# Low parts of the first MLP weights on another engine, modulation dots at other steps, and another form of the last squares and the final norm

## The chip, the cores and the metric

The kernel runs on one core of a Trainium2 chip. The metric is the device time of one execution in microseconds (us). The kernel before the change was timed three times: 2294.85, 2296.27 and 2297.2 us, median **2296.27 us**.

A core has engines that work beside one another, each through its own queue of instructions in order: TensorE (PE: matmuls; PEld: its weight loads), VectorE (DVE: elementwise work), ScalarE (ACT: activations, copies, scalings), GpSimd (POOL: elementwise work) and SyncE (SP), from whose queue the DMA transfers here are issued.

## The reference

A trunk of two layers over one sequence of 1024 tokens with 1024 channels, all in float32. The first layer mixes tokens by latent attention, the second by an mLSTM; each is followed by a gated MLP. Cut to what the change touches:

```python
D_MODEL, SEQ, DEPTH, D_FF, CONV_W = 1024, 1024, 2, 2816, 3
c_act = jax.nn.silu(c)
for i in range(DEPTH):
    mod = c_act @ mod_w[i] + mod_b[i]              # 6 x 1024 numbers
    sh_a, sc_a, g_a, sh_f, sc_f, g_f = split(mod, 6)
    h = rms_norm(x) * (1 + sc_a) + sh_a
    y = mla_mixer(h, ...) if i % 2 == 0 else mlstm_mixer(h, ...)
    x = x + g_a * y
    h = rms_norm(x) * (1 + sc_f) + sh_f
    x = x + g_f * conv_ffn(h, ffn_w_up[i], ffn_conv_w[i], ffn_conv_b[i], ffn_w_down[i])
return rms_norm(x, final_norm)                      # gain of 1024 numbers

def conv_ffn(h, w_up, conv_w, conv_b, w_down):
    a, g = split(h @ w_up, 2)                       # 2 x 2816 channels
    a = causal depthwise convolution of width 3 over tokens (a) + conv_b
    return (gelu(a) * g) @ w_down
```

## The kernel before

**Layout.** Activations lie transposed: 128 channels on the partitions, 8 tiles (KT) for the 1024 channels, and the tokens in two halves of 512 (HS). `x` is the residual stream, `h` the normed and modulated input of an MLP.

**Products.** Every float32 product is made of three matmuls (`mm3`, L174, with its matmuls on L178, L179 and L180): high part of the weight by high part of the operand, high by low, low by high. A weight is split by `wop` (L943): ACT copies it into `whi` (L948), and then DVE or POOL subtracts this from the weight into `wlo` (L949); the caller names the engine.

**The MLP's up projection** (`mlp`, L925). The 22 tiles of channels are 22 groups `g`. Each group computes its two halves (a, before the convolution, and g, the gate) for both halves of tokens in seven products instead of eight, in the manner of Strassen. A product is a step `k` of 12 matmuls, with the function that makes its weight and the function that runs it in the table `steps`. Its operands are B11 and B21 (parts of `h` itself), B22, and T1 to T4 (sums and differences of parts of `h`, made by `operands_second`, whose DVE rows are on L886, in two steps of 128x1024). The steps:

- 1: weight straight from the loaded tile `ra`, into the bank `pa`, copied into `a1` by ACT;
- 2: weight `ra` (second half), added into `a1` by DVE;
- 5: weight the sum `s` (L962), into the bank `pd`, copied by ACT into `g2` (L1017);
- 3: weight a difference `t` (L966 and L967), into `pd`, copied into `a2`;
- 6: weight `s` itself, onto `pa`, added by DVE into `a2` (L1029); the convolution `conv` (ACT L988, DVE L989 and L990, ACT L991) follows;
- 7: weight another difference `t` (L971), onto `pa`, added by DVE into `g2` (L1036);
- 4: weight from the loaded tile `rg`, onto `pa`, out.

The first four groups (`g["again"]`, AHEAD = 4) are run apart: first steps 1 and 2 of all four, for which `h` of the first half of tokens is enough, then, by pairs of groups, steps 5, 3, 6, 7 and 4, which need the T operands. The other 18 groups follow one another in the order 5, 1, 7 of the group before, 2, 4 of the group before, 3, 6. This is the loop; a list `seq` holds all steps of an MLP (28 for the first four groups, 126 for the rest), and the weight of a step is made some steps ahead of its product. Before the change the low parts of steps 1, 2, 4, 6 and 7 are made on POOL, those of 3 and 5 on DVE, in all groups. The loaded weight tiles `raw` have 4 buffers, the tiles `wraw` with `s` and `t` have 2. Rows called `wsum` are parts of the latter.

**The modulation's dots.** Both layers' modulation is a product of a vector with a matrix. Row tiles of `mod_w` of 512 KB are loaded on SP's queue (L214, two buffers `mraw`), and DVE multiplies each by `crow` with an accumulated sum (`mod_dot`, L202), one column of the result each. Some of these dots are fed into the first MLP by its hook `extra`, called with the number `i` of the step: one dot at every third step, from step 0 to step 144.

**The down projection** (`d_run`, L1146) runs seven products per group in the same manner into the banks `da` and `db`; `gate_x` (L287, row L291) adds each result with its gate into `x` on DVE. In the last group the squares of the finished tiles are summed (`Squares`, L222: ACT squares, DVE adds, L240). The last product of the last group is done in one piece of 512 columns in the first MLP, and in two pieces of 256 columns in the second one.

**The norms.** `rstd_later` (L262) counts matmul triples (`mm3` counts down a list): after a first number of triples, `rstd_cols` (L242) sums the squares over the channels by small matmuls with ones (`st`, one per 128 tokens, L247), DVE scales them (`var`, L251), and POOL takes them to the power -1/2 (L252); after a second number, `to_rows` (L255) spreads the result over the partitions by four transposes (`rb`, L259). Then a function of the caller uses `rb`: `norm_mod` makes `h` of the second layer (a DVE row `nt`, an ACT row, a DVE row per tile), `final` makes the output: one DVE instruction per tile of 128 channels (L1600, x times `fn`, the final norm's gain, times `rb`), and one store on SP's queue for each two tiles. For the final norm the two pairs of numbers are WF = (6, 22) and WF_RSTD = (5, 8), each for the first and the second half of tokens.

**What sets the order.** The functions issue instructions in program order, and a scheduler with priorities places them on the engines; those in `tc.high_priority()` go ahead of what else is ready.

## Time and profile before

| | before |
|---|---|
| median of three timed runs | 2296.27 us |
| the profiled execution's own time | 2297.02 us |
| its span on the core | 2295.3 us |
| its mean granted TensorE clock | 0.979 of full speed |
| HBM read, written | 220.49 MB, 44.47 MB |
| ACT `whi` L948 of `raw` tiles and others, x252 | 146.4 us |
| POOL `wlo` L949 of `raw` tiles, x228 | 341.6 us, 1507 ns each |
| DVE `wlo` L949, x136 | 104.5 us, 773 ns each |

How to read it: busy times are the sums of an engine's instructions in the profiled execution, and the engines overlap. A row with "[7 <-POOL wlo]" says that the engine stood for 7 us ahead of that instruction, until POOL had made `wlo`. In rows, out<-in names the tile that is written and those that are read, then the shape on 128 partitions, and xN counts instructions. Windows are counted in us from the start of the span. The rows on which the prediction rests stand in it.

### The profile page before, as it was taken

The numbers are of one execution on the slowest core, as the hardware profiler recorded it, in microseconds if no ns is written. First come the engines' busy times: TensorE is split into PE (matmuls) and PEld (weight loads), VectorE is DVE, ScalarE is ACT, GpSimd is POOL, SyncE is SP. The second block draws the span as 40 slices with busy tenths as digits, with TensorE's granted clock in tenths as the row PEclk, the third lists the DMA queues.
The fourth block names the chain that finished last, engine by engine and source line by source line (L and its number), as shares of the span: only waits on it lengthen the run. The fifth ranks groups of instructions, "written<-read, shape, count | busy, mean of one in ns | idle before, by whom it ended". The sixth has DMA issues, their size and how long they took to land. (4 is left out here: it accounts for less than half of the span.)

```text
span 2295.3 us, 28811 instructions
## 1 busy us (share of the span) xinstructions
PE 2198.5 (96%) x10489; PEld 1824.8 (80%) x10489; DVE 1698.2 (74%) x2457; ACT 1023.6 (45%) x1784; POOL 756.3 (33%) x550
## 2 busy tenths in 40 slices
PE   8989999998999999999999999999899999999997
PEld 6778888886788888777878878978678888877786
DVE  7876777679988888899972634365776666679987
ACT  5355555445444444443443423344544444453332
POOL 3221111243443343432233222234543333342222
PEclk9999999999999999999999999999999999999998
DMA  7411334762554444642122111135242222245122
GB/s 290 146 47 61 105 98 134 264 204 79 183 161 151 147 147 147 202 147 85 59 97 79 56 46 56 33 125 174 62 128 91 88 83 83 83 151 210 48 74 74
DMA packets 104830, 269.46 MB, mean 117 GB/s; under 512 B 12208, under 2 KB 15984, under 8 KB 104688
## 3 DMA queue, kind: packets, MB, share of 16 engines
q1 hardware_dynamic: 104688, 267.62, 35.8%
q8 instruction: 83, 1.36, 0.3%
q14 instruction: 59, 0.48, 0.1%
HBM read 220.49 MB, written 44.47 MB: 115 GB/s over the span
## 5 line engine op out<-in xcount | busy, mean ns | idle before, releaser
L949 POOL TENSOR_TENSOR wlo<-raw,whi 128x512 fp32r<-128x512 f32 (+1 forms) x228 | 341.6, 1507 | 563.8 <-ACT whi L948 556.6
L171 POOL TENSOR_TENSOR wlo<-wraw,whi 128x1024 fp32r<-128x1024 f32 x64 | 156.4, 2448 | 303.5 <-ACT whi L170 253.2
L948 ACT ACTIVATE whi<-raw 128x512 fp32r<-128x512 f32 (+1 forms) x252 | 146.4, 604 | 220.5 <-PE pb L179 54.5
L949 POOL TENSOR_TENSOR wlo<-wsum,whi 128x512 fp32r<-128x512 f32 x88 | 153.6, 1748 | 245.9 <-ACT whi L948 245.9
L180 PE MATMUL pa<-T,wlo 128*128 128x512 f32 x528 | 207.5, 394 | 14.5 <-POOL wlo L949 14.5
L178 PE MATMUL pa<-T,whi 128*128 128x512 f32 x528 | 208.2, 395 | 9.1 <-DVE a L1029 5.3
L179 PE MATMUL pa<-T,whi 128*128 128x512 f32 x528 | 207.6, 394 | 0.7 <-DVE T L886 0.7
L948 ACT ACTIVATE whi<-wsum 128x512 fp32r<-128x512 f32 (+1 forms) x224 | 134.7, 617 | 163.4 <-PE pa L179 50.3
L178 PE MATMUL da<-U,whi 128*128 128x512 f32 (+1 forms) x364 | 140.7, 386 | 3.2 <-DVE x L291 3.2
L179 PE MATMUL da<-U,whi 128*128 128x512 f32 (+1 forms) x364 | 139.9, 384 | 0.0
L180 PE MATMUL da<-U,wlo 128*128 128x512 f32 (+1 forms) x364 | 139.3, 384 | 0.0
L180 PEld LDWEIGHTS pa<-T,wlo 128*128 128x128 f32 x528 | 99.7, 189 | 37.7 <-POOL wlo L949 15.3
L178 PEld LDWEIGHTS pa<-T,whi 128*128 128x128 f32 x528 | 99.6, 189 | 35.6 <-DVE g L1036 4.6
L170 ACT ACTIVATE whi<-wraw 128x1024 fp32r<-128x1024 f32 x67 | 70.7, 1059 | 126.3 <-PE op L179 53.1
L988 ACT ACTIVATE ct<-a,cols 128x512 f32<-128x512 f32 x88 | 70.9, 811 | 124.6 <-DVE a L1010 70.9
L949 DVE TENSOR_TENSOR wlo<-wsum,whi 128x512 fp32r<-128x512 f32 (+1 forms) x136 | 104.5, 773 | 19.6 <-ACT whi L948 18.6
L179 PEld LDWEIGHTS pa<-T,whi 128*128 128x128 f32 x528 | 99.3, 188 | 23.1 <-DVE T L886 1.6
L991 ACT ACTIVATE ct<-ct 128x512 f32<-128x512 f32 x88 | 55.5, 631 | 127.3 <-DVE ct L990 127.2
L1098 DVE TENSOR_TENSOR U<-q,U 128x1024 fp32r<-128x1024 f32 x84 | 104.1, 1258 | 6.4 <-ACT U L1097 5.7
L180 PE MATMUL db<-U,wlo 128*128 128x512 f32 x264 | 103.1, 392 | 1.7 <-DVE wlo L949 1.7
L178 PE MATMUL db<-U,whi 128*128 128x512 f32 x264 | 103.8, 393 | 0.0
L179 PE MATMUL db<-U,whi 128*128 128x512 f32 x264 | 103.1, 391 | 0.0
(361 smaller groups left out, 6380.6 us busy)
## 6 DMA issues: line engine op xcount, KB each, us to landing
raw<-in_wf SPq DMA_DIRECT2D x96, 512.0 KB, 4.0
wraw<-in_w SPq DMA_DIRECT2D x67, 512.0 KB, 3.6
mraw<-in_mod_w SPq DMA_DIRECT2D x56, 512.0 KB, 4.3
ud<-ct SPq DMA_DIRECT2D x88, 256.0 KB, 2.6
q<-ud SPq DMA_DIRECT2D x88, 256.0 KB, 4.4
raw<-in_wd SPq DMA_DIRECT2D x32, 512.0 KB, 6.2
pa<-in_mod_w SPq DMA_DIRECT2D x24, 512.0 KB, 3.8
xd<-x SPq DMA_DIRECT2D x48, 256.0 KB, 2.7
```

The source lines that it names most:

```text
L170: act.activation(hi, raw, AF.Copy)
L171: (lo_eng or pool).tensor_tensor(lo, raw, hi.bitcast(F32), ALU.subtract)
L178: pe.matmul(ps, lh, rh, start=first, stop=False, skip_group_check=more)
L179: pe.matmul(ps[:, 0:rl.shape[-1]], lh, rl, start=False, stop=False, skip_group_check=more)
L180: pe.matmul(ps, ll, rh, start=False, stop=last, skip_group_check=more)
L948: act.activation(hi, src, AF.Copy)
L949: eng.tensor_tensor(lo, src, hi.bitcast(F32), ALU.subtract)
L988: act.activation(t, a[:, 2:], AF.Identity, bias=col(f"cb{l}", m), scale=cw(m, 2))
L991: act.activation(t, t, AF.Gelu)
L1098: dve.tensor_tensor(lo, w, hi.bitcast(F32), ALU.subtract)
```

## The change

It has four parts.

1. In the four first groups of each MLP, the subtractions for the low parts of steps 4, 6 and 7 are given to DVE instead of POOL: three per group, 12 per MLP, 24 in all. Those of steps 1 and 2, and all of the loop's, stay where they were.
2. In the first MLP the dots are fed in at every second step from step 41 on, instead of at every third from step 0 on. 49 dots take the steps 41 to 137.
3. The last square of the last group (tile 7 of each half of tokens, in both MLPs) is no longer added to the sum by DVE; `Squares.keep` lets it stand, and `rstd_cols` sums it by a second set of small matmuls that accumulates onto the first. All squares of that group are issued with high priority.
4. The final norm's gain `fn` is multiplied into each tile of `x` by ACT (`gain`) right behind its square. `final` then has one DVE instruction for two tiles, x times `rb` broadcast, and a store behind it. The counts WF and WF_RSTD become (4, 8) and (4, 8), and OUTS goes.

```diff
-W0, W0_RSTD, WF, WF_RSTD = (6, 10), (4, 3), (6, 22), (5, 8)
+W0, W0_RSTD, WF, WF_RSTD = (6, 10), (4, 3), (4, 8), (4, 8)
-OUTS = 2
...
+            self.more = []
+
+        def keep(self, x):
+
+            sq = self.sq()
+            act.activation(sq, x, AF.Square)
+            self.more.append(sq)
...
         for t in range(nt):
-            pe.matmul(st[:, t:t + 1], ssq.t[:, t * P:(t + 1) * P], ones, start=True, stop=True)
+            terms = [ssq.t, *ssq.more]
+            for i, v in enumerate(terms):
+                pe.matmul(st[:, t:t + 1], v[:, t * P:(t + 1) * P], ones, start=i == 0, stop=i == len(terms) - 1)
...
         def w_s3(g):
             dve.tensor_tensor(g["t"], g["ra"][:, 0:HS], g["rg"][:, 0:HS], ALU.subtract)
-            return wop(g["t"], pool)
+            return wop(g["t"], dve if g["again"] else pool)
...
+        def eng(g):
+
+            return dve if g["again"] else pool
+
         steps = {1: (w_a, p1), 2: (lambda g: wop(g["ra"][:, HS:], pool), p2), 3: (w_s4, p3),
-                 4: (lambda g: wop(g["rg"][:, HS:], pool), p4), 5: (w_s1, p5), 6: (lambda g: wop(g["s"], pool), p6),
-                 7: (w_s3, p7)}
+                 4: (lambda g: wop(g["rg"][:, HS:], eng(g)), p4), 5: (w_s1, p5),
+                 6: (lambda g: wop(g["s"], eng(g)), p6), 7: (w_s3, p7)}
...
-                        stats[hf, c0].add(xs[hf][:, m, c0:c0 + cw_])
+                        with tc.high_priority():
+                            if p == 3 and op in ("T3", "T4"):
+                                stats[hf, c0].keep(xs[hf][:, m, c0:c0 + cw_])
+                            else:
+                                stats[hf, c0].add(xs[hf][:, m, c0:c0 + cw_])
+                        if scaled is not None:
+                            scaled(xs[hf][:, m, c0:c0 + cw_], m)
...
-    mlp(px, psC, T, 0, u_d[0], pD, done, ((0, HS),), lambda i: piece(mods, i % 3 == 0))
+    mlp(px, psC, T, 0, u_d[0], pD, done, ((0, HS),), lambda i: piece(mods, i >= 40 and i % 2))
...
+    def gain(x, m):
+        act.activation(x, x, AF.Copy, scale=col("fn", m))
+
     def final(x, hf, t0, w, rb):
+
         x = x[:, :, t0:t0 + w]
-        for k in range(KT):
-            dve.scalar_tensor_tensor(x[:, k, :], x[:, k, :], col("fn", k), rb[:, 0:w], ALU.mult, ALU.mult)
-            if k % OUTS == OUTS - 1:
-                k0 = k - OUTS + 1
-                o0 = hf * HS + t0
-                nc.sync.dma_start(out[k0:k + 1, :, o0:o0 + w].rearrange("k p t -> p k t"), x[:, k0:k + 1, :])
+        for k in range(0, KT, 2):
+            v = x[:, k:k + 2, :]
+            dve.tensor_tensor(v, v, rb[:, 0:w].unsqueeze(1).to_broadcast([P, 2, w]), ALU.mult)
+            o0 = hf * HS + t0
+            nc.sync.dma_start(out[k:k + 2, :, o0:o0 + w].rearrange("k p t -> p k t"), v)
...
-    mlp(px, psC, T, 1, u_d[1], pD, done, ((0, 256), (256, 256)))
+    mlp(px, psC, T, 1, u_d[1], pD, done, ((0, 256), (256, 256)), None, gain)
```

The first place is at the T operands of the first MLP, where the first pair of groups goes from step 5 to the steps 3 and 6. DVE's instructions before the change (`T_935` and `T_964` are operands of later steps, `mraw` the dots, `wsum_5119` and `wsum_5192` the sums and differences of the first two groups, `wlo_5215` the low part for step 3):

```order
L886 TENSOR_TENSOR T_935_5020<-x_4670,T_935_5020 128x1024
L202 SCALAR_TENSOR_TENSOR mraw_5066,modc_80<-mraw_5066,crow 128x1024
L949 TENSOR_TENSOR wlo_5215<-wsum_5119,whi_5214 128x512
L886 TENSOR_TENSOR T_964_5168<-x_4106,T_964_5168 128x1024 x2
L967 TENSOR_TENSOR wsum_5192<-raw_5188,wsum_5192 128x512
L971 TENSOR_TENSOR wsum_5119<-raw_5115,raw_5117 128x512
L202 SCALAR_TENSOR_TENSOR mraw_5253,modc_80<-mraw_5253,crow 128x1024
L949 TENSOR_TENSOR wlo_5215<-wsum_5192,whi_5214 128x512
```

And DVE's instructions there in the changed kernel (line numbers are shifted: L886 is L894 now, L949 is L957, L967 is L975, L971 is L979; `wlo_5210` is the low part for step 3, `wlo_5248` that for step 6):

```order
L894 TENSOR_TENSOR T_935_5020<-x_4670,T_935_5020 128x1024
L957 TENSOR_TENSOR wlo_5210<-wsum_5117,whi_5209 128x512
L975 TENSOR_TENSOR wsum_5187<-raw_5183,wsum_5187 128x512
L894 TENSOR_TENSOR T_963_5166<-x_4106,T_963_5166 128x1024 x2
L957 TENSOR_TENSOR wlo_5210<-wsum_5187,whi_5209 128x512
L957 TENSOR_TENSOR wlo_5248<-wsum_5117,whi_5247 128x512
L957 TENSOR_TENSOR wlo_5248<-wsum_5187,whi_5247 128x512
L979 TENSOR_TENSOR wsum_5117<-raw_5113,raw_5115 128x512
```

The dots are gone from here, and two more subtractions stand ahead of L979 (L971 before), the difference for step 7: those of step 6, which POOL made. On PE, at the same place, the products of steps 3 and 6 stood so (`pd` with `B_933`, the operand B22, is step 3; `pa` with `T_934`, the operand T2, is step 6, whose low part `wlo_5256` POOL makes):

```order
L178 MATMUL pa_5050<-T_934_5019,whi_5255 128x512
L178 MATMUL pa_5090<-T_934_5019,whi_5255 128x512
L179 MATMUL pa_5050<-T_934_5019,whi_5255 128x512
L179 MATMUL pa_5090<-T_934_5019,whi_5255 128x512
L180 MATMUL pa_5050<-T_934_5019,wlo_5256 128x512
L180 MATMUL pd_5275<-B_933_5018,wlo_5215 128x512
```

In the changed kernel:

```order
L177 MATMUL pa_5050<-T_934_5019,whi_5247 128x512
L177 MATMUL pa_5088<-T_934_5019,whi_5247 128x512
L178 MATMUL pa_5050<-T_934_5019,whi_5247 128x512
L178 MATMUL pa_5088<-T_934_5019,whi_5247 128x512
L179 MATMUL pd_5267<-B_933_5018,wlo_5210 128x512
L177 MATMUL pd_5267<-B_933_5018,whi_5209 128x512
```

The first matmul there that needs a low part was one of step 6, with `wlo` of POOL; now it is one of step 3, with `wlo` of DVE.

The second place is the loop of the first MLP on DVE, between the add into `a` (L1029, now L1037) and the add into `g` (L1036, now L1044). Before:

```order
L1029 TENSOR_TENSOR a_6386<-a_6386,pa_6293 128x512
L989 SCALAR_TENSOR_TENSOR ct_6409<-a_6386,cols_4405,ct_6409 128x512
L990 SCALAR_TENSOR_TENSOR ct_6409<-a_6386,cols_4405,ct_6409 128x512
L202 SCALAR_TENSOR_TENSOR mraw_6351,modc_80<-mraw_6351,crow 128x1024
L949 TENSOR_TENSOR wlo_6461<-wsum_6458,whi_6460 128x512
L966 TENSOR_TENSOR wsum_6458<-wsum_6458,raw_6482 128x512
L967 TENSOR_TENSOR wsum_6458<-raw_6482,wsum_6458 128x512
L1036 TENSOR_TENSOR g_1115_6284<-g_1115_6284,pa_6293 128x512
```

In the changed kernel, in a later group:

```order
L1037 TENSOR_TENSOR a_6811<-a_6811,pa_6715 128x512
L957 TENSOR_TENSOR wlo_6864<-wsum_6888,whi_6863 128x512
L201 SCALAR_TENSOR_TENSOR mraw_6842,modc_80<-mraw_6842,crow 128x1024
L997 SCALAR_TENSOR_TENSOR ct_6836<-a_6811,cols_4405,ct_6836 128x512
L974 TENSOR_TENSOR wsum_6888<-wsum_6888,raw_6907 128x512
L998 SCALAR_TENSOR_TENSOR ct_6836<-a_6811,cols_4405,ct_6836 128x512
L201 SCALAR_TENSOR_TENSOR mraw_6795,modc_80<-mraw_6795,crow 128x1024
L975 TENSOR_TENSOR wsum_6888<-raw_6907,wsum_6888 128x512
L970 TENSOR_TENSOR wsum_7039<-raw_7037 128x512
L1044 TENSOR_TENSOR g_1169_6708<-g_1169_6708,pa_6715 128x512
```

There are two dots (L202, now L201) between the two adds in place of one, and the sum of the next group (L970, formerly L962) stands there too.

The third place is DVE at the end of the program, behind the last gated adds. Before:

```order
L291 SCALAR_TENSOR_TENSOR x_17066<-da_18273,modc_80,x_17066 128x256
L251 TENSOR_SCALAR var_18757<-st_18754 128x2
L1600 SCALAR_TENSOR_TENSOR x_17097<-x_17097,cols,rb_18623 128x512 x6
L240 TENSOR_TENSOR ssq_18565<-ssq_18565,sq_18725 128x256
L240 TENSOR_TENSOR ssq_18565<-ssq_18565,sq_18738 128x256
L240 TENSOR_TENSOR ssq_18565<-ssq_18565,sq_18751 128x256
L251 TENSOR_SCALAR var_18764<-st_18761 128x2
L1600 SCALAR_TENSOR_TENSOR x_17066<-x_17066,cols,rb_18768 128x256 x8
L1600 SCALAR_TENSOR_TENSOR x_17066<-x_17066,cols,rb_18783 128x256 x8
```

In the changed kernel:

```order
L1623 TENSOR_TENSOR x_17103<-x_17103,rb_18627 128x1024
L259 TENSOR_SCALAR var_18765<-st_18760 128x2
L299 SCALAR_TENSOR_TENSOR x_17072<-da_18261,modc_80,x_17072 128x256
L246 TENSOR_TENSOR ssq_18579<-ssq_18579,sq_18750 128x256
L299 SCALAR_TENSOR_TENSOR x_17072<-da_18279,modc_80,x_17072 128x256
L246 TENSOR_TENSOR ssq_18579<-ssq_18579,sq_18773 128x256
L1623 TENSOR_TENSOR x_17103<-x_17103,rb_18627 128x1024 x2
L1623 TENSOR_TENSOR x_17072<-x_17072,rb_18790 128x2x256 x4
```

`x_17097` (now `x_17103`) is the first half of tokens, `x_17066` (now `x_17072`) the second. Six output rows stood ahead of the last added squares; now the adds come first, and the rows of two tiles follow.

More of the change, by code (lines that the diff above doesn't have):

```diff
@@ L923, in operands_second, with mlp @@
             split_two(T["T4"], k, two(x1, k))
-    def mlp(px, psC, T, l, u_d, pd, done, cols, extra=None):
+    def mlp(px, psC, T, l, u_d, pd, done, cols, extra=None, scaled=None):
         cw = lambda m, j: col(f"cw{l}", m * 3 + j)
```

## Prediction

> **What bounds the kernel now.** First the page's first part, then the waits of TensorE (PE) in total: in us, times, longest.
>
> ```profile
> PE 2198.5 (96%) x10489; PEld 1824.8 (80%) x10489; DVE 1698.2 (74%) x2457; ACT 1023.6 (45%) x1784; POOL 756.3 (33%) x550
> PE pa L180 <- POOL wlo L949: 14.5, 2, 7.3
> PE pd L178 <- ACT g L1017: 1.9, 1, 1.9
> ```
>
> PE sets the time; only its gaps can be won. The largest wait comes twice, once in each MLP, for a low part that POOL computes. Windows tell how much is lost in all around the two places (PE busy with its matmuls in brackets, PEld, DVE, ACT, POOL, granted clock, DMA share, GB/s); the last two rows are the loops of the first and the second MLP.
>
> ```profile
> 540.00:610.00 70.00, 56.15 (x221) 43.63 (x222) 66.85 (x86) 30.89 (x48) 31.42 (x17) 0.90 0.47 154
> 1650.00:1720.00 70.00, 61.40 (x249) 49.37 (x250) 54.83 (x71) 32.75 (x52) 34.33 (x21) 0.90 0.36 113
> 610.00:900.00 290.00, 289.48 (x1264) 236.35 (x1263) 239.41 (x314) 123.80 (x212) 114.29 (x91) 1.00 0.49 154
> 1720.00:2010.00 290.00, 290.00 (x1267) 237.38 (x1266) 196.85 (x243) 124.74 (x212) 108.27 (x90) 1.00 0.27 85
> ```
>
> In a loop a matmul takes 290/1267 = 0.229 us, so 70 us would hold 306. The first window lacks 85 of them (19.5 us), the second 57 (13.0 us). That is all there is to win there. The loops lose nothing, but DVE is busy for 83% of the first one and 68% of the second: the difference is the modulation's dots.
>
> **Why PE waits there.** POOL's, DVE's and PE's rows of the timeline around both waits:
>
> ```profile
> 533.72 14.69 POOL L949 TENSOR_TENSOR wlo<-wsum,whi 128x512 fp32r<-128x512 f32 x2 [15.29 <-ACT whi L948]
> 1643.23 15.30 POOL L949 TENSOR_TENSOR wlo<-wsum,whi 128x512 fp32r<-128x512 f32 x2 [15.28 <-ACT whi L948]
> 543.24 1.22 DVE L886 TENSOR_TENSOR T<-x,T 128x1024 fp32r<-128x1024 f32 x1
> 544.37 1.22 DVE L202 SCALAR_TENSOR_TENSOR mraw<-mraw,crow 128x1024 f32<-128x1024 f32 x1
> 545.52 1.75 DVE L949 TENSOR_TENSOR wlo<-wsum,whi 128x512 fp32r<-128x512 f32 x1
> 1653.89 0.69 DVE L949 TENSOR_TENSOR wlo<-wsum,whi 128x512 fp32r<-128x512 f32 x1
> 546.77 0.79 PE L180 MATMUL pa<-T,wlo 128*128 128x512 f32 x1 [7.21 <-POOL wlo L949]
> 1656.36 0.80 PE L180 MATMUL pa<-T,wlo 128*128 128x512 f32 x1 [7.27 <-POOL wlo L949]
> L949 POOL TENSOR_TENSOR wlo<-wsum,whi 128x512 fp32r<-128x512 f32 x88 | 153.6, 1748 | 245.9 <-ACT whi L948 245.9
> ```
>
> POOL needs 14.7 and 15.3 us for two subtractions that take 1.75 us each on average, while DVE works through its operands (T, B) without a gap. [...]
>
> **The first weights, first MLP.** In the order PE now asks first for the low part of pd, which DVE computes right behind its operands: at 544.37, where the dot stood, plus 0.69 is 545.05, and PE goes on 1.7 us earlier than 546.77. So most of the wait stays: it was POOL's by name, but DVE's queue lies just below it. What remains of the lost 19.5 us is 545.05 - 540 = 5.05 and the slow restart:
>
> ```profile
> 548.00:552.00 4.00, 3.86 (x11) 0.56 0.16 61
> 1692.00:1696.00 4.00, 4.00 (x12) 0.63 0.82 260
> ```
>
> At a clock of 0.56 the four us hold 11 matmuls in place of 17.5, 1.5 us lost; with the stretch before, 2.0. So at most 19.5 - 5.05 - 2.0 = 12.4 us can be won. Behind the wait DVE gets 12 subtractions (three kinds in four groups) at 0.61 us from start to start, 7.3 us, and loses the nine dots up to 610, 13.9 us:
>
> ```profile
> L202 DVE SCALAR_TENSOR_TENSOR mraw<-mraw,crow 128x1024 f32<-128x1024 f32 x9 | 13.9, 1549 | 0.0
> 594.95 0.47 PE L178 MATMUL pa<-T,whi 128*128 128x512 f32 x1 [3.56 <-DVE a L1029]
> ```
>
> Following DVE's rows one by one from 545.05, its add into a is done about 4 us before PE's third product needs it in the second pair of groups: the wait of 3.56 goes, and with it its slow restart. I take **11 us**; lower bound 1.7, the first step alone.
>
> **The first weights, second MLP.** Here DVE's part is done at 1653.89 + 0.69 = 1654.58, again 1.8 us before 1656.36. Of 13.0 us there remain 1654.58 - 1650 = 4.6 and 2.0 of slow restart, so at most 6.4. No dot leaves here and DVE gets 7.3 us more; but its rows beside POOL's (1.7 to 1.8 us for 0.7) shorten, and the wait for g of 1.9 us, whose ACT copy stands behind such a row, should go with its restart at 0.63. Against this, DVE must wait for one weight tile whose buffer its own later subtraction frees (about 0.5 us on PE). I take **5.5 us**; lower bound 1.5.
>
> [...]
>
> **The dots in the first loop.** They now come at every second step from the 41st, not every third from the first. So 49 of them lie in 97 steps of 2.74 us (12 matmuls):
>
> ```profile
> L202 DVE SCALAR_TENSOR_TENSOR mraw<-mraw,crow 128x1024 f32<-128x1024 f32 x36 | 47.7, 1326 | 0.0
> L990 DVE SCALAR_TENSOR_TENSOR ct<-a,cols,ct 128x512 f32<-128x512 f32 x30 | 27.9, 930 | 0.6
> L989 DVE SCALAR_TENSOR_TENSOR ct<-a,cols,ct 128x512 f32<-128x512 f32 x30 | 26.6, 885 | 8.4 <-ACT ct L988 8.4
> L949 DVE TENSOR_TENSOR wlo<-wsum,whi 128x512 fp32r<-128x512 f32 x30 | 24.1, 803 | 5.8 <-ACT whi L948 5.7
> L967 DVE TENSOR_TENSOR wsum<-raw,wsum 128x512 f32<-128x512 f32 x16 | 18.7, 1170 | 0.3
> L962 DVE TENSOR_TENSOR wsum<-raw 128x512 f32<-128x512 f32 x15 | 15.8, 1052 | 23.4 <-POOL wlo L949 23.4
> L966 DVE TENSOR_TENSOR wsum<-wsum,raw 128x512 f32<-128x512 f32 x15 | 12.5, 832 | 0.8 <-DMA raw<-in_wf 0.3
> L1029 DVE TENSOR_TENSOR a<-a,pa 128x512 f32<-128x512 f32 x15 | 10.2, 680 | 3.4 <-PE pa L180 3.4
> L1036 DVE TENSOR_TENSOR g<-g,pa 128x512 f32<-128x512 f32 x14 | 9.6, 683 | 3.6 <-PE pa L180 3.6
> ```
>
> In 290 us that is 53 in place of 36, 17 x 1.33 = 23 us more, so DVE goes from 239 to 262 us, 90%. What hides them is DVE's idle time, 51 us, most of it before wsum. The close place is between the adds into a (L1029) and g (L1036): PE spends four steps, 11.0 us, from the end of the product before the one to the start of the product behind the other. In every second group two dots now lie there; at the means above (L1029, L949, dot, L989, L966, L990, dot, L967, L962, L1036, as the order has them) DVE needs 9.7 us. It fits by 1.3 us, less what DVE waits within. I take **1 us lost**, bounds 0 and 7 (seven such groups, 1 us each). SP gets each dot's load of 512 KB closer; DMA share 0.49 would be some 0.55.
>
> **The last squares.** Where PE sums kept squares there are eight small matmuls in place of four:
>
> ```profile
> 1158.87 1.05 PE L247 MATMUL st<-ones,ssq 128*128 128x1 f32 x8 [0.23 <-DVE ssq L240]
> 1159.79 0.48 PE L178 MATMUL db<-U,whi 128*128 128x512 f32 x1
> ```
>
> Four cost 1159.79 - 1158.87 = 0.92 us, so each norm at the end of the first MLP costs PE 0.9 more, against the 0.23 won. The adds now stand ahead of half of the first half's rows (nt, h), which delays h by up to 3 us with 2.4 in hand. Together **1.5 us lost** (0 to 3).
>
> **The tail.**
>
> ```profile
> 2274.27 0.65 PE L259 MATMUL rb<-ident,rstd 128*128 128x128 f32 x4 [0.76 <-POOL rstd L252]
> 2277.36 0.41 PE L180 MATMUL da<-U,wlo 128*128 128x256 f32 x1
> 2278.53 4.03 DVE L1600 SCALAR_TENSOR_TENSOR x<-x,cols,rb 128x512 f32<-128x512 f32 x6
> 2284.01 1.01 PE L247 MATMUL st<-ones,ssq 128*128 128x1 f32 x4 [5.59 <-DVE ssq L240]
> 2285.58 6.36 DVE L1600 SCALAR_TENSOR_TENSOR x<-x,cols,rb 128x256 f32<-128x256 f32 x16 [0.30 <-PE rb L259]
> 519.89 2.35 DVE L879 TENSOR_TENSOR x<-x,rb 128x1024 f32<-128x1024 f32 x2
> 2280.00:2284.00 4.00, 0.00 (x0) 0.00 (x0) 3.74 (x7) 0.42 (x1) 0.00 (x0) 0.50 0.78 296
> 2288.00:2292.00 4.00, 0.00 (x0) 0.00 (x0) 3.94 (x11) 0.00 (x0) 0.00 (x0) 0.50 1.02 332
> ```
>
> Six output rows stand ahead of the last squares on DVE, hence the 5.59; this order goes. DVE's rows: 8 x 0.67 + 16 x 0.40 = 11.7 us become 4 x 1.14 (by L879, two tiles against PSUM) + 8 x 0.67 = 9.9. But PE gets 0.9 for the first st, and a doubled st (1.7 to 2.0 at half clock, by the row of 1.01) between the last products, so these end at 2280.3, not 2277.6. Then the gate (0.5), the add and one double row (1.5) pass beside the last square and its doubled st, which end at 2283.5; two double rows (2.3) and eight (5.4) end at 2291.2, and the store behind takes as before 2295.3 - 2291.94 = 3.4: 2294.6. The stores alone end little earlier: with the second pair of tiles out at 2282.9, 1.5 MB at 296 / 0.78 = 380 GB/s and 2 MB at 332 need 10.4 us, to 2293.3. **0.7 us won** (3 won to 1.5 lost). The gains are put on by ACT, which works 0.4 of 4 us here.
>
> **Sum**, against the profiled execution's 2297.02: -11 - 5.5 + 1 + 1.5 - 0.7 = -14.7, 2282.3. It stands 0.75 over the median of 2296.27, so the forecast is 2281.6.
>
> **The rivals.** A: *DVE takes the place of POOL.* The waits move to DVE's queue, and only the first steps (1.7 + 1.8) and a bit of the rest are won: -6 + 2, about 2292. For it: DVE is busy for 66.85 of the 70 us of the first window. Against it: 13.9 us of dots leave there. B: *the dots make DVE the bound of the first loop.* Beside POOL a row of DVE can take twice its time (1.75 above for 0.69). If each of the 53 dots takes twice its undisturbed 1.22, DVE needs 239 - 48 + 129 = 320 us in 290; it decides from dots of 1.86 on. PE then loses 30 us, and 2281.6 + 29 = 2311, slower. For it: more DVE rows beside POOL's. Against it: the mean dot stays at 1.33 with POOL busy for 39% of this loop. C: *nothing arrives*, as the weights' DMAs behind the freed buffers come late and give back both places: about 2295. Against it: DMA share 0.47 and 0.36 there, and the dots' loads no longer stand ahead of the weights' in SP's queue, where they hold it for 34 us:
>
> ```profile
> 511.90 34.06 SPq L214 DMA_DIRECT2D mraw<-in_mod_w  x3
> ```
>
> **Chances.** Forecast 0.68, A 0.16, C 0.07, B 0.09. The range takes A in and the larger bounds of the forecast (12.4 + 6.4 + 3 won, nothing lost): 2274.5 to 2292. A change of less than 0.2% (4.6 us) can hardly be told from none. Faster by more than that, under 2291.7: the forecast and near three quarters of A, 0.80; same: the rest of A, C and a mild B, 0.13; slower 0.07.
>
> **What would show it.** In the new profile PE waits for DVE's wlo, not POOL's, 5 to 6 us at 545 and at 1640; no wait for a of 3.6 us; POOL without a row of 14 us; the dots between 620 and 905 with no PE wait over 1 us; the tail's last DVE row some 11 us behind the last product, and stores back to back. A PE wait in each second group of the first loop means B; waits for wlo or raw between 550 and 590 mean A or C.

## The result and the profile after

The changed kernel takes **2314.74 us**, median of seven runs (2305.38 to 2319.17), against 2296.27 us before (seven runs, 2291.38 to 2300.8): ratio 1.0074, 95% interval 1.0052 to 1.0097. It is 0.7% slower, which lies outside the range of 2274.5 to 2292 us and goes against the forecast of 2281.6 us.

The profiled execution has a span of 2314.4 us, 19.1 more than before. The page's first part and PE's largest waits (us in total, times, longest) of the changed kernel:

```profile
PE 2210.5 (96%) x10521; PEld 1836.4 (79%) x10521; DVE 1686.2 (73%) x2464; ACT 1036.7 (45%) x1808; POOL 692.1 (30%) x526
PE pa L177 <- DVE g L1044: 24.8, 8, 3.9
PE pd L179 <- DVE wlo L957: 11.1, 2, 5.5
```

The wait for POOL's low part (14.5 us before) has become one for DVE's, 11.1. A new one stands above it: PE waits for the add into g. The windows of the changed kernel (PE with matmuls, PEld, DVE, ACT, POOL, clock, DMA share, GB/s) show where: the first weights of both MLPs, counted from the same place as before, then the loops.

```profile
542.00:612.00 70.00, 64.56 (x274) 52.44 (x275) 59.03 (x90) 35.85 (x57) 11.05 (x10) 0.95 0.37 122
1677.00:1747.00 70.00, 65.32 (x273) 52.94 (x274) 58.10 (x89) 35.85 (x57) 10.72 (x10) 0.95 0.35 121
620.00:910.00 290.00, 268.36 (x1121) 217.02 (x1121) 226.21 (x309) 109.39 (x186) 104.70 (x82) 0.96 0.49 155
1749.00:2039.00 290.00, 290.00 (x1268) 237.43 (x1267) 197.98 (x244) 124.49 (x212) 108.42 (x90) 1.00 0.27 86
```

In 70 us the first weights now hold 274 and 273 matmuls in place of 221 and 249. But the first loop lost 143 of its 1264, and DVE is busy there for 226 of 290 us, less than the 239 before: it is not full, it waits.

The whole by stages, from DVE's rows in the timeline: from the first low part of B22 to the fifth add into g ("first weights"), from there to the last add into g ("loop"), then to the first ACT row of `C` in the mLSTM, and the second MLP in the same way. In us:

| kernel | first weights 1 | loop 1 | to C | first weights 2 | loop 2 | to the end | median |
|---|---|---|---|---|---|---|---|
| before | 98.5 | 326.7 | 309.8 | 92.5 | 325.7 | 236.3 | 2296.27 |
| changed | 85.9 | **359.2** | 313.3 | 87.0 | 325.7 | 233.9 | 2314.74 |
| e1 dots as before | 91.8 | 326.7 | 313.3 | 87.0 | 325.7 | 234.3 | 2287.7 |
| e2 loads one dot ahead | 86.2 | 356.2 | 313.3 | 87.0 | 325.7 | 233.9 | one run |
| e3 sum on POOL | 86.3 | 339.1 | 313.3 | 88.0 | 325.7 | 233.9 | one run |
| e4 dots spread | 86.4 | 328.2 | 316.7 | 86.8 | 325.7 | 233.9 | 2284.92 |
| e5 sums' tiles taken once | 86.0 | 332.5 | 309.6 | 86.9 | 325.7 | 233.9 | one run |
| e6 half dots | 85.9 | 333.4 | 314.8 | 86.9 | 325.7 | 233.9 | one run |
| e7 dots in order | 87.6 | 332.8 | 312.8 | 86.9 | 325.7 | 233.9 | one run |
| e8 no loads | 86.4 | 332.7 | 311.3 | 87.3 | 325.7 | 233.8 | one run |
| e9 = e4, squares as before | 86.4 | 328.2 | 313.4 | 87.2 | 325.7 | 233.9 | 2281.0 |
| e10 = e9 with e5's tiles | 86.2 | 327.0 | 313.1 | 86.0 | 325.7 | 237.1 | 2279.4 |
| e11 before, dots moved | 90.3 | 349.4 | 309.6 | 92.5 | 325.7 | 236.2 | one run |

The differences of the changed kernel to before, taken before rounding: -12.6, **+32.6**, +3.5, -5.5, 0 and -2.5. With +2.3 up to the first weights and +1.2 between C and the second MLP this makes the 19.1. One stage turned a gain of some 14 us into a loss of 19.

Each row of stages comes from one execution, and executions of the changed kernel differ by up to 14 us. The second loop repeats to 0.1 us in all thirteen kernels, and the first weights of the first MLP to 1.7 us in the ten that have the whole change there. But the part ahead of them took 527.6 to 533.8 us in eight kernels whose differences all lie behind it. So a few us outside the loops and the first weights say little by themselves.

**The place.** It lies between DVE's add into a and its add into g. It comes once in two groups, six times in the loop: 43.5 to 44.7 us for two groups instead of 38.4. DVE's rows of the timeline of the changed kernel at the first of them (start, us, then in brackets the idle time ahead and its releaser; the rows that close the accumulation of a dot are left out):

```profile
667.73 1.21 DVE L201 SCALAR_TENSOR_TENSOR mraw<-mraw,crow 128x1024 f32<-128x1024 f32 x1
...
670.19 0.68 DVE L1037 TENSOR_TENSOR a<-a,pa 128x512 f32<-128x512 f32 x1
670.79 1.19 DVE L957 TENSOR_TENSOR wlo<-wsum,whi 128x512 fp32r<-128x512 f32 x1
674.01 1.23 DVE L201 SCALAR_TENSOR_TENSOR mraw<-mraw,crow 128x1024 f32<-128x1024 f32 x1 [2.04 <-DMA mraw<-in_mod_w]
675.16 0.75 DVE L997 SCALAR_TENSOR_TENSOR ct<-a,cols,ct 128x512 f32<-128x512 f32 x1
675.83 0.68 DVE L974 TENSOR_TENSOR wsum<-wsum,raw 128x512 f32<-128x512 f32 x1
676.43 0.74 DVE L998 SCALAR_TENSOR_TENSOR ct<-a,cols,ct 128x512 f32<-128x512 f32 x1
677.09 1.22 DVE L201 SCALAR_TENSOR_TENSOR mraw<-mraw,crow 128x1024 f32<-128x1024 f32 x1
678.23 0.69 DVE L975 TENSOR_TENSOR wsum<-raw,wsum 128x512 f32<-128x512 f32 x1
681.33 1.74 DVE L970 TENSOR_TENSOR wsum<-raw 128x512 f32<-128x512 f32 x1 [2.41 <-POOL wlo L957]
682.99 0.67 DVE L1044 TENSOR_TENSOR g<-g,pa 128x512 f32<-128x512 f32 x1
```

PE's row behind it, which waits for that add:

```profile
683.81 0.77 PE L177 MATMUL pa<-T,whi 128*128 128x512 f32 x1 [3.84 <-DVE g L1044]
```

Read it from the add into a (670.19) to the end of the add into g (683.66): 13.5 us, of which DVE works 9.0 (forecast: 9.7) and waits 2.04 + 2.41 = 4.45. PE gives 11.0 us between the products, and DVE begins on the add into a about 1.2 us after PE has finished, since a dot, a low part and a difference stand ahead of it. So 11.0 - 9.0 - 1.2 - 4.45 = -3.7, and PE's waits at the six places are 3.25 to 3.85 us. Before the change, the stretch with one dot had the wait for POOL too, and still fitted: from 640.84 to 650.93 it took 10.1 us, of which 2.95 were waits, and PE did not wait. Its last two rows:

```profile
649.64 0.69 DVE L962 TENSOR_TENSOR wsum<-raw 128x512 f32<-128x512 f32 x1 [2.69 <-POOL wlo L949]
650.25 0.68 DVE L1036 TENSOR_TENSOR g<-g,pa 128x512 f32<-128x512 f32 x1
```

The first wait is a matter of order. The rows of the change that were shown ahead of the prediction have it in the numbers of the tiles: `mraw_6842` stands ahead of `mraw_6795`. Of the two dots, the one whose load was issued later runs first, and waits for that load, while the other's has landed. The second wait hangs on it: behind the late dot comes the convolution (L998), ACT's gelu waits for that at the head of ACT's queue, and ACT's copies of the weights and POOL's low part behind it. ACT's and POOL's rows there:

```profile
677.21 0.63 ACT L999 ACTIVATE ct<-ct 128x512 f32<-128x512 f32 x1 [4.86 <-DVE ct L998]
678.74 0.62 ACT L956 ACTIVATE whi<-wsum 128x512 fp32r<-128x512 f32 x1
680.04 1.25 POOL L957 TENSOR_TENSOR wlo<-wsum,whi 128x512 fp32r<-128x512 f32 x1
```

POOL is done at 681.29, and L970, which overwrites what POOL reads, starts at 681.33. Behind each of PE's six waits the clock falls as well. Windows of the changed kernel around the wait of 3.40 us that ends at 859.05:

```profile
854.00:858.00 4.00, 1.65 (x8) 1.03 (x6) 1.58 (x2) 1.75 (x4) 4.00 (x4) 0.96 0.44 131
858.00:862.00 4.00, 2.95 (x7) 2.40 (x8) 3.97 (x8) 0.82 (x1) 1.47 (x2) 0.50 0.34 86
862.00:866.00 4.00, 4.00 (x13) 3.13 (x13) 2.35 (x5) 0.00 (x0) 0.00 (x0) 0.69 0.65 246
```

So a place costs 5.1 to 6.3 us: the wait and the slow restart. The clock stands at 0.50 for 3.41 us behind five of the waits and for 6.83 us at this one. Each 3.41 us at 0.50 are put at 1.7 us lost (half of them, an estimate; behind the wait that ends at 727.29 the matmuls then start 0.43 us apart, ahead of it 0.23). In all that is 21.6 us of waits and 11.1 us lost to the slow clock behind them, 32.8 together, where before PE waited for 0.5 us at full clock: 32.2 of the loop's 32.6 us.

### The profile page after: what moved, and what is told of

Read it like the earlier page. It is cut to its first block, busy times and chain, and to the rows that moved or that the text cites. A ratio compares the mean times of both kernels' runs of the same rounds, so it can differ in the third digit from the quotient of the medians.

```text
span 2314.4 us, 28836 instructions
## 1 busy us (share of the span) xinstructions
PE 2210.5 (96%) x10521; PEld 1836.4 (79%) x10521; DVE 1686.2 (73%) x2464; ACT 1036.7 (45%) x1808; POOL 692.1 (30%) x526
## 5 line engine op out<-in xcount | busy, mean ns | idle before, releaser
L957 POOL TENSOR_TENSOR wlo<-raw,whi 128x512 fp32r<-128x512 f32 (+1 forms) x220 | 327.0, 1496 | 590.0 <-ACT whi L956 580.6
L177 PE MATMUL pa<-T,whi 128*128 128x512 f32 x528 | 211.3, 401 | 24.8 <-DVE g L1044 24.8
L178 PE MATMUL pa<-T,whi 128*128 128x512 f32 x528 | 210.3, 399 | 0.7 <-DVE T L894 0.7
L957 POOL TENSOR_TENSOR wlo<-wsum,whi 128x512 fp32r<-128x512 f32 x72 | 103.8, 1441 | 206.1 <-ACT whi L956 202.0
L957 DVE TENSOR_TENSOR wlo<-wsum,whi 128x512 fp32r<-128x512 f32 (+1 forms) x152 | 112.2, 748 | 28.1 <-ACT whi L956 27.2
L178 PE MATMUL inp<-h,whi 128*128 128x512 f32 x256 | 103.1, 403 | 3.2 <-DVE h L283 3.2
L177 PE MATMUL db<-U,whi 128*128 128x512 f32 x264 | 103.5, 392 | 0.0
```

The costliest lines, as they stand in the source:

```text
L177: pe.matmul(ps, lh, rh, start=first, stop=False, skip_group_check=more)
L178: pe.matmul(ps[:, 0:rl.shape[-1]], lh, rl, start=False, stop=False, skip_group_check=more)
L957: eng.tensor_tensor(lo, src, hi.bitcast(F32), ALU.subtract)
```

## The experiments

Three theories were held against one another. **W**: DVE is late by the sum of its work and its waits between the two adds. **D**: two dots there are too much work in themselves (the prediction's rival B, in a milder form). **L**: the closer loads of 512 KB hurt by their traffic.

**e1, the dots back.**

```diff
-    mlp(px, psC, T, 0, u_d[0], pD, done, ((0, HS),), lambda i: piece(mods, i >= 40 and i % 2))
+    mlp(px, psC, T, 0, u_d[0], pD, done, ((0, HS),), lambda i: piece(mods, i % 3 == 0))
```

> The changed kernel with the dots back at every third step from step 0. The loop of the first MLP, from the fifth to the last add into g, took 326.7 us before and 359.2 us after the change. If the dots' places alone lengthen it, it is 326 to 329 us again. If the subtractions on DVE had a part in it (they end 9 us ahead of it), it stays above 335 us. The first weights (start of the B22 operands to the fifth add into g) took 98.5 us before and 86.0 us after: if the nine dots that left this place brought most of the 12.5 us, they now take 93 us or more, and if the subtractions brought most, 90 us or less. Whole time in the first case about 2288 to 2292 us, in the second 2280 to 2286 us.

The loop is at 326.7 us again: without the dots' new places it is not longer. The first weights take 91.8 us, between the two bounds: the subtractions brought 6.7 of the 12.6 us, the dots' leaving 5.9. The whole is 2287.7 us, 0.3 under what was expected in this case, ratio 0.9968 (0.9954 to 0.9982).

**e2, the loads one dot ahead.** The generator of the dots holds two loads under way.

```diff
+        load()
+        load()
+        yield
+        while raws:
+            j, k, raw = raws.pop(0)
+            tc.keep_in_program_order(mod_dot(l, j * 8 + k, raw))
+            load()
```

> The changed kernel, but each dot's load is issued one dot earlier (two loads under way in the same two buffers); DVE's work and the places of the dots stay. Theory W (waits): in every second group a dot waits 2 us for its load, ACT's gelu behind it holds up the high parts of the weights, POOL's low part comes late, and the sum for the next group (L970), which waits 2.4 us for POOL, holds up the add into g. Without the late load this chain runs about 2 us earlier: PE's wait for g falls from 3.5 us to 1.5 us or to none, and the loop from 359 us to 327 to 345 us. Theory D (work): two dots more than fit between the two adds, whatever they wait for: the loop stays at 355 us or more. Theory L (traffic): closer loads of 512 KB delay the weights' loads: the loop stays, and waits for raw tiles show.

It missed: 356.2 us. But the experiment did not take the wait away. DVE's row at one place, and two of SP's:

```profile
755.15 1.23 DVE L201 SCALAR_TENSOR_TENSOR mraw<-mraw,crow 128x1024 f32<-128x1024 f32 x1 [1.81 <-DMA mraw<-in_mod_w]
744.06 0.33 SPq L1261 DMA_DIRECT2D mraw<-in_mod_w  x1
750.34 0.33 SPq L1261 DMA_DIRECT2D mraw<-in_mod_w  x1
```

The load issued at 744.06 landed at 747.64; the dot waited for the one of 750.34, which landed at 755.13. The two dots stand swapped here too. Neither theory is decided by it.

**e3, the sum on POOL.**

```diff
-            dve.tensor_tensor(g["s"], g["rg"][:, 0:HS], g["rg"][:, HS:], ALU.add)
+            (dve if g["again"] else pool).tensor_tensor(g["s"], g["rg"][:, 0:HS], g["rg"][:, HS:], ALU.add)
```

> The changed kernel, but in the loop of both MLPs the sum s (L970) is made on POOL, so that DVE no longer waits there for POOL's low part; loads and dots stay. Theory W: g's add comes 2.4 us of waiting and 1.7 us of work earlier, more than PE's wait of 3.5 us, so that PE waits for g no longer or less than 0.5 us each time, and the loop is 327 to 333 us. Theory D: only 0.7 to 1.7 us of work leave each place, PE still waits about 2 us, and the loop is 343 us or more. A third way: POOL, with one instruction more per group, becomes late itself, and PE waits for POOL's low parts.

The waits for g are 0.33 to 0.44 us, as W has it, but the loop is 339.1 us and misses the 327 to 333 of W, since PE now also waits for the add into a, up to 1.8 us. PE does not wait for a low part of POOL there, so the third way did not come about. The sum and its wait were a part of the loss; a dot that waits for its load now holds up the other add (3.50 us at 728.82, ahead of the add at 730.57).

**e4, the dots spread.**

```diff
-    mlp(px, psC, T, 0, u_d[0], pD, done, ((0, HS),), lambda i: piece(mods, i >= 40 and i % 2))
+    mlp(px, psC, T, 0, u_d[0], pD, done, ((0, HS),), lambda i: piece(mods, i >= 36 and (i - 33) % 7 in (2, 4, 6)))
```

> The changed kernel with three dots in each group of seven steps from step 37 on, at steps 3, 5 and 7 of each group's seven, so that only one dot lies between the add into a and the add into g, as before the change; the number of dots in the loop stays at about 50. Theories W and D: no wait for g, the loop is 326 to 330 us, and the whole time is that of the changed kernel less 30 to 33 us, about 2280 to 2285 us, faster than the kernel before. Theory L (the denser loads themselves cost): the loop stays above 335 us.

The loop is 328.2 us with as many dots (44) in the window of 290 us. The window holds all its matmuls, with DVE busy for 250 us, 24 more than in the changed kernel, and with more DMA. The window of e4:

```profile
620.00:910.00 290.00, 290.00 (x1262) 235.97 (x1261) 250.41 (x335) 125.76 (x212) 111.55 (x90) 1.00 0.52 164
```

That rules L out, and DVE's total as a bound. The whole is 2284.92 us, ratio 0.9959 (0.9945 to 0.9973).

**e5, the sums' tiles taken once per MLP.**

```diff
-            t = wp.tile([P, 1024], F32, tag="wraw", bufs=wraws, name=nm("wsum"))
+            if len(pair) < 2:
+                pair.append(wp.tile([P, 1024], F32, tag="wraw", bufs=wraws, name=nm("wsum")))
+            t = pair[g["m"] % 2]
```

> The changed kernel, but the two tiles of sums and differences are taken once per MLP and used by turns, so that the sum s (L970 of the changed kernel) waits only for the reader of the old s, a whole group earlier, and no longer for POOL's low part of the old difference; DVE's order and work, dots and loads stay. Theory W (DVE is late by the sum of its work and its waits between the two adds, less a slack of 1.3 us): the 2.4 us of waiting and the 1.0 us by which L970 is slow beside POOL go, so PE's wait for g falls from 3.5 us to between 0 and 1.1 us, and the loop (fifth to last add into g, 359.2 us in the changed kernel, 326.7 before) is 327 to 338 us. Theory D (two dots' work there is too much in itself): PE still waits over 2 us, the loop stays at 350 us or more.

332.5 us, as W has it: with two whole dots, the wait for a load (0.7 to 1.75 us) and the same order of rows, the loop loses 5.8 us in place of 32.6. The sum itself did not get shorter (1.78 us), though that had been expected. DVE's rows of e5, where the sum (L974 there) no longer waits:

```profile
674.55 0.69 DVE L979 TENSOR_TENSOR wsum<-raw,wsum 128x512 f32<-128x512 f32 x1
675.16 1.78 DVE L974 TENSOR_TENSOR wsum<-raw 128x512 f32<-128x512 f32 x1
676.86 0.67 DVE L1048 TENSOR_TENSOR g<-g,pa 128x512 f32<-128x512 f32 x1
```

**e6, half dots.**

```diff
+        n = 512 if l else D
-        return dve.scalar_tensor_tensor(raw, raw, 1.0, crow, ALU.mult, ALU.mult, accum_out=modc[l][:, i:i + 1])
+        return dve.scalar_tensor_tensor(raw[:, 0:n], raw[:, 0:n], 1.0, crow[:, 0:n], ALU.mult, ALU.mult, accum_out=modc[l][:, i:i + 1])
```

> The changed kernel with the dots of the second layer over 512 instead of 1024 columns (half of each sum is left out, the loads stay whole): the order and the waits stay, DVE's work at each place falls by 2 x 0.6 us. Theory W: PE's wait for g falls from 3.5 us by 1.2 us to about 2.3 us, the loop from 359 to 347 to 353 us. Theory D: the work is what counts, 1.2 us less of it with nothing else changed brings the loop to 335 us or less.

333.4 us: by its number this is D's forecast and a miss of W's. DVE's rows of e6 at one place tell why that does not speak for D:

```profile
749.63 0.69 DVE L202 SCALAR_TENSOR_TENSOR mraw<-mraw,crow 128x512 f32<-128x512 f32 x1 [1.56 <-DMA mraw<-in_mod_w]
...
752.18 0.69 DVE L202 SCALAR_TENSOR_TENSOR mraw<-mraw,crow 128x512 f32<-128x512 f32 x1
752.79 0.69 DVE L976 TENSOR_TENSOR wsum<-raw,wsum 128x512 f32<-128x512 f32 x1
756.10 0.69 DVE L971 TENSOR_TENSOR wsum<-raw 128x512 f32<-128x512 f32 x1 [2.62 <-POOL wlo L958]
756.71 0.68 DVE L1045 TENSOR_TENSOR g<-g,pa 128x512 f32<-128x512 f32 x1
```

The waits are still there (1.56 and 2.62). Besides the 1.1 us of the two dots, the sum takes 0.69 us instead of the 1.74 that it took in the changed kernel beside a POOL row (681.26 to 682.51), and the add into a begins 0.1 us behind PE's product in place of 1.2, as the dots ahead of it are halved too. Against this, DVE's waits and its subtraction behind the add are some 0.5 us longer. So PE's wait falls by 2.6 us on average in place of 1.2. PE's waits are 0.71 to 1.72 us, none of which was followed by a slow restart (behind the longest the matmuls start 0.23 us apart), so that a place costs about 1 us and no longer 5.4. W's sum comes out with these terms, but it was made without two of them, so this run alone does not decide between W and D; e5 and e7 do, which keep both whole dots.

**e7, the dots in the order of their loads.**

```diff
-                tc.keep_in_program_order(mod_dot(l, j * 8 + k, raw))
+                tc.keep_in_program_order(dve.scalar_tensor_tensor(junk[0], raw, 1.0, crow, ALU.mult, ALU.mult, accum_out=modc[1][:, i:i + 1]))
```

> The changed kernel, but each dot writes its products to one common tile of bfloat16, which keeps the dots in the order of their loads; in the changed kernel two of them stand swapped between the two adds, so that DVE waits 2 us for the load of the later one while that of the earlier one has long landed. Their places within the stretch change with this: both dots now stand behind the convolution's two rows. Theory W: the wait of 2.0 us for the load goes, ACT's gelu, its copies of the weights and POOL's low part come 3 us earlier, and with them L970: PE's wait for g is below 1 us, the loop 327 to 336 us. Theory D: two dots stand there still, the loop stays at 350 us or more.

332.8 us, W's forecast: two whole dots stand there, and DVE's rows of e7 show no wait for a load:

```profile
673.71 1.22 DVE L1263 SCALAR_TENSOR_TENSOR junk<-mraw,crow 128x1024 bf16<-128x1024 f32 x1
...
674.97 1.23 DVE L1263 SCALAR_TENSOR_TENSOR junk<-mraw,crow 128x1024 bf16<-128x1024 f32 x1
...
678.62 0.69 DVE L970 TENSOR_TENSOR wsum<-raw 128x512 f32<-128x512 f32 x1 [2.42 <-POOL wlo L957]
679.23 0.68 DVE L1044 TENSOR_TENSOR g<-g,pa 128x512 f32<-128x512 f32 x1
```

L970 still waits 2.42 us for POOL, but takes 0.69 us instead of 1.74. The place is shorter by the 2.0 us of the wait for the load and by this 1.0 us. What is left, 6.1 us in the loop, are six waits of 0.9 us and little more.

**e8, no loads.**

```diff
+                if len(raws) < 2:
+                    raws.append(pF[0].tile([P, D], F32, tag="mraw", bufs=2, name=nm("mraw")))
+                    nc.sync.dma_start(raws[-1], mod_w[1, j * 8 + k])
```

> As the one with the dots in order, but all dots of the second layer read two tiles that are loaded once: 46 of the 48 loads of 512 KB are left out, so the modulation is wrong. DVE's order and work are the same. Theory W: as with the dots in order, within 5 us in the loop. Theory L (the loads' traffic delays the weights): the loop is shorter here by 10 us or more than with the dots in order. Theory D: the loop stays at 350 us or more in both.

332.7 us, the same as e7 to 0.1: the traffic of the dots' loads costs nothing in the loop. L is out.

**e9, the squares of the first MLP as before**, on top of e4.

```diff
+                        if l:
                             with tc.high_priority():
...
+                        else:
+                            stats[hf, c0].add(xs[hf][:, m, c0:c0 + cw_])
```

> The kernel with the dots spread (e4), and in the first MLP the last squares as before the change: added on DVE, no high priority, four small matmuls; in the second MLP they stay changed. From the last add into g of the first MLP to the first ACT row of C in the mLSTM it took 309.8 us before, 313.3 us in the changed kernel and 316.7 us in e4. If the kept squares and their priority cost this, it is 309 to 311 us, and the whole time 3 to 6 us below e4's 2284.9 us, 2279 to 2282 us. If not, it stays at 313 us or more and the time is e4's.

The stage to C stays at 313.4 us, so the kept squares alone are not what makes it longer; the next section takes it apart. The whole is 2281.0 us, ratio 0.9936 (0.9919 to 0.9953), which lies in the range expected if the squares were the cause; that it is better than e4 is not shown, as their intervals overlap.

**e10, e9 with e5's tiles.**

> e9 with the sums' tiles taken once (e5) as well: the loop of the first MLP took 328.2 us with the dots spread alone, 326.7 before the change. Theory W: without the wait for POOL nothing is late between the two adds, 326.5 to 327.5 us, so the whole is 1 us better than e9 at most, 2278 to 2282 us. If the tile's release has another use (weights earlier elsewhere, as the 309.6 us of e5 between the loop and C might tell), 2275 to 2279 us.

The loop is 327.0 us, its shortest with the dots moved. The whole is **2279.4 us** (six runs), ratio 0.9922 (0.9906 to 0.9937), against 2296.94 for the kernel before on the same chip: the best version of this study. That it is better than e9 is not shown, their intervals overlap. In its profiled execution the end is 3.2 us longer than in e9. The edit does not touch that part; what made the difference is open.

**e11, the kernel before with only the dots moved.**

> The kernel before with only the dots moved to every second step from step 41 on. If the dots' places alone lengthen the loop, it is 352 to 360 us (326.7 before), whatever DVE and POOL share at the first weights. The first weights took 98.5 us before, 91.8 with the subtractions on DVE alone (e1), 85.9 with both: the dots' leaving alone should give 90 to 95 us if the two gains add up, and stay above 96 us if POOL's low part is what is waited for there.

The loop is 349.4 us, under the 352 to 360 that were expected. The same two waits of DVE (1.80 and 2.42 us at the first) stand at its places, but two of the six waits of PE are only 1.8 and 1.9 us long, and the clock was halved behind three of the six: 17.5 us of waits and 5.0 us lost to the slow clock, of 22.8 us lost in all. So the dots' places are enough to lengthen the loop. The dots' leaving alone brings 8.2 us at the first weights. With the subtractions' 6.7 that would be 14.9; both together bring 12.6, so the two parts overlap by 2.3 us.

## Why the prediction was wrong

**The first weights, first MLP: right.** Forecast 11 us won, measured 12.6. The first matmul with a low part starts at 547.44 behind a wait of 5.55 us for DVE, as forecast, no wait for a is left, and POOL has no row there any more. The bound of 12.4 was worked out from matmuls in the window, and by these (53 more, 12.1 us) it held.

**The first weights, second MLP: right.** 5.5 us forecast, 5.5 measured.

**The dots in the first loop: this step failed.** "It fits by 1.3 us, less what DVE waits within. I take 1 us lost, bounds 0 and 7" became 32.6 us. The place and DVE's work there were right (9.7 us forecast, 9.0 measured). The waits within were named ("less what DVE waits within") and not priced, and they were 4.45 us at the first place, 3.9 to 4.5 at the six. Both could be seen: the wait of wsum for POOL stood in a row that the prediction quotes (23.4 us idle, seven waits of 2.7 to 3.8), and the swapped dots stood in the quoted order. The prediction read DVE's idle time of 51 us as room, "most of it before wsum"; those 23.4 us are under half of it, and they are a wait for POOL that stands ahead of the add into g whether DVE has room or not. The late start of 1.2 us was not thought of. And the bound of 7 us took each place for 1 us, when each place was late by over 3 us and lost 1.6 to 2.7 us to the slow clock on top.

**Rival B was right by its place and sum, wrong by its mechanism.** It gave 30 us lost if dots took twice their time. Its 2311 us lies near the measured 2314.74 by luck. The dots did not take that long: the groups of DVE in the changed loop show a mean of 1.39 us, below B's threshold of 1.86, beside the 18.3 us of waiting ahead of the sum:

```profile
L201 DVE SCALAR_TENSOR_TENSOR mraw<-mraw,crow 128x1024 f32<-128x1024 f32 x44 | 61.2, 1390 | 10.9 <-DMA mraw<-in_mod_w 10.9
L970 DVE TENSOR_TENSOR wsum<-raw 128x512 f32<-128x512 f32 x14 | 17.0, 1212 | 18.3 <-POOL wlo L957 18.3
```

DVE was never the bound of the loop by its total; it was late at one place. Means and shares of busy time, on which B's chance of 0.09 was argued, could not tell.

**The last squares and the norm: 1.5 us forecast, 3.5 measured to C, by another way.** The rows for h come late, as forecast: PE's waits for them grew from 0.9 to 3.2 us. But the waits for rstd fell from 3.0 to 0.3, more than the 0.23 us put down as won, and all of PE's waits in this stage together hardly changed: 10.1 us, 9.9 before. What differs is the clock: it is at 0.50 for 10.2 us of the stage, for 3.4 before. Half of these 6.8 us more, 3.4, is nearly all of the 3.5. e5, with the kept squares and the same wait for h, has 3.4 us at 0.50, as before, and takes 309.6 us in all. e9, without the kept squares, waits 3.0 us for rstd again and comes to its 313.4 us otherwise: by 2.2 us more of waits than before, most of them for h, where three rows take 2.15 to 2.90 us for 0.74, and by 1.7 us more of slow clock. What the doubled small matmuls cost by themselves is not shown.

**The tail: 0.7 us forecast, 2.5 won.** The last ten output rows and the stores of the changed kernel:

```profile
2301.72 7.12 DVE L1623 TENSOR_TENSOR x<-x,rb 128x1024 f32<-128x1024 f32 x10
2297.98 12.82 SPq L1625 DMA_DIRECT2D out<-x  x12
```

DVE ends at 2308.84, 5.6 us ahead of the end instead of 3.4: the stores set the end now, as the second way of working it out had it.

Without the loop's step the forecast would have held: e4 and e9, which have all of the change but the place of the dots (e9 less its first squares), run at 2284.92 and 2281.0 us. That they come so near is partly luck: more was won than forecast at the first weights and in the tail, and more was lost to C.

## What to carry to other kernels

Work that is moved into an engine's idle time must be laid against one deadline at a time, and the sum there must hold the waits of the instructions ahead, not their work alone: an engine that is busy for 78% was late six times by over 3 us. An order of instructions is also to be read for what each row needs: two loads taken in the wrong order are seen in it before anything runs. And a deadline missed by 0.9 us cost 1 us here; one missed by over 3 us cost 5 to 6 in the changed kernel, since PE's clock was halved behind it (at all six such places there, and at three of the four in e11).

## What the runs showed of the hardware

The clock did not answer to the length of a wait alone. The trace's record of the granted clock has two values, 1.00 and 0.50, in the kernel before and in the changed kernel. Between 540 and 2200 us each stretch at 0.50 lasts 3.41 us or two or three times that in both, and the starts lie on one grid of 3.41 us: in the changed kernel 683.57, 727.94, 772.32 and 816.69 are 13 steps apart each. What went with the slow clock there is how long PE stood idle within one step of that grid: 1.72 to 3.41 us in the step ahead of each of the 22 stretches, and at most 1.79 us in any step at 1.00 that another one at 1.00 followed. The wait of 1.88 us in the kernel before, which ends at 1690.18, lies within one step, and the next step is halved:

```profile
1688.13:1691.54 3.41, 1.53 (x7) 1.14 (x7) 0.93 (x2) 2.64 (x5) 1.82 (x2) 1.00 0.00 0
1691.54:1694.95 3.41, 3.41 (x10) 2.64 (x9) 0.10 (x1) 0.79 (x2) 0.71 (x1) 0.50 0.81 241
1694.95:1698.36 3.41, 3.41 (x17) 2.78 (x16) 3.34 (x4) 0.85 (x2) 1.42 (x1) 1.00 0.18 71
```

But behind a wait of 3.42 us in e11, which ends at 810.39, the matmuls start 0.23 us apart as at full clock; the grid, taken from the slow matmuls of that run, cuts it into some 1.6 and 1.8 us. Behind one of 1.80 us there (768.21) the clock stayed at 1.00, and so it did in e2 behind one of 3.50 us, which ends at 809.68. The window of e2:

```profile
808.00:812.00 4.00, 2.32 (x10) 1.97 (x11) 3.96 (x5) 0.76 (x1) 2.10 (x3) 1.00 0.13 50
```

How much of a step must be idle is not shown: 1.72 us in the step from 1524.29 on in the kernel before was followed by the slow clock, 1.79 in the one from 809.86 on in the changed kernel was not.

So waits of the same length cost differently. PE's row behind the late h in the changed kernel and its windows:

```profile
1202.46 0.80 PE L178 MATMUL inp<-h,whi 128*128 128x512 f32 x1 [2.37 <-DVE h L283]
1203.00:1207.00 4.00, 4.00 (x17) 3.56 (x15) 1.47 (x3) 1.38 (x2) 0.00 (x0) 0.50 0.33 123
1207.00:1211.00 4.00, 4.00 (x13) 3.42 (x14) 2.67 (x5) 1.28 (x2) 1.45 (x1) 0.50 0.00 0
```

The same in e5:

```profile
1172.71 0.50 PE L178 MATMUL inp<-h,whi 128*128 128x512 f32 x1 [2.36 <-DVE h L283]
1173.00:1177.00 4.00, 4.00 (x24) 3.59 (x24) 2.78 (x6) 1.38 (x2) 0.81 (x1) 0.82 0.37 131
1177.00:1181.00 4.00, 4.00 (x14) 3.10 (x14) 2.50 (x4) 1.38 (x2) 0.64 (x1) 0.75 0.01 2
```

The eight us behind it hold 30 matmuls in the one and 38 in the other. In the changed kernel 2.31 us of the wait lie in one step of the grid, and three steps are halved; in e5 it is cut into 1.81 and 0.55, and one step is halved. The two steps more are 3.4 of the 3.8 us by which the two kernels differ to C.

What a row of DVE takes beside POOL shows again in single rows: in the changed kernel the sum of two weight tiles (L970) took 1.73 to 1.78 us in all 17 rows that had POOL rows beside them for more than half of their time, and 0.68 to 0.69 in the 25 without one. The row at 681.33 took 1.74.
